# Loading each raw weight block one step ahead, in front of the W12 loads, in the seven-product stretches

## The chip, the cores and the metric

One core of one Trainium2 chip runs the kernel. The metric is the device time of one execution in microseconds, as a median of several runs. A profiled execution gives the trace that the rows below come from. TensorE is called PE here, VectorE DVE, ScalarE ACT, GpSimd POOL and SyncE SP. SP computes nothing: it issues nearly all loads, in the order in which they are written for it, and an instruction that has to wait holds up those behind it.

## The reference, cut to what matters

Two layers over 512 tokens of width 2048: a latent-attention layer and an mLSTM layer. The change touches the input projection of the second alone:

```python
proj = x @ w_in                      # x (512, 2048), w_in (2048, 8208), float32
qk, v, o, gates, z = jnp.split(proj, [o1, o2, o3, o4], axis=-1)
...
return (hcell * jax.nn.silu(z)) @ w_out
```

`v` (values), `o` and `z` (two gates) are 2048 columns wide each. Two of the four 512-column blocks of `v`, and all of `o` and `z`, come out of the function that the diff changes.

## The kernel before, in words

**Arithmetic.** A float32 product is made from three products of a shorter format. `split` (L166) cuts a tile into a high part, copied by ACT (L168), and a low part, which DVE gets by subtraction (L169). `mm3` (L206) then issues high x high, high x low and low x high, each a 128x128 by 128x512 matmul at L203.

**Seven products for eight.** `quad` (L298) computes 512 tokens by two 512-column blocks, c0 and c1, in the manner of Strassen and Winograd. The 2048 rows of the weights are taken in pairs of 128-row blocks, an even and an odd one. W11 is the even block at c0, W12 the even one at c1, W21 and W22 the odd ones at c0 and c1. Seven products (q1 to q7) of these, or of sums of these, with sums of the tokens' blocks replace eight. It is called five times in a row: once for `v`, then for each of four pairs of `o` and `z` blocks. In the time of the trace the five calls run from 819.6 to 1225.7 us.

**Stretches and steps.** A call has three stretches, each a loop over `i` = 0, 2, 4, 6, so of four steps. A step loads one raw block (`raw`, L315 to L320: 128 x 1024 floats, 512 KB, issued at L319) and works on it:

- first stretch (L355 to L363): W11 is the raw block. DVE adds W12 to it into a tile `t` (L360, two halves). q1 takes the split of W11, q5 that of `t`. `right` (L322 to L328) loads W12 as two tiles `e` of 256 KB (L327).
- second stretch (L371 to L379): W22 is the raw block, and W12 is loaded again. DVE adds W22 to W12 in place (L374, two halves) and to `t` (L376, two halves). q7 takes the split of the first sum, q6 that of `t`, q3 that of W22.
- third stretch (L398 to L404): W21 is the raw block. DVE adds it to `t` (L401, two halves). q2 takes the split of W21, q4 that of `t`. No W12 here.

A product of one step is 12 matmuls, so a step is 24, 36 or 24 matmuls, and a call 336.

**Buffers.** There are three raw buffers (`N_RAW`, L43), three of high and of low parts (`N_HI`), four `e` tiles (`N_E`, L42), hence room for the W12 of two steps, and 16 `t` tiles. A raw buffer comes free when its split at L169 and the additions that read it are done; an `e` tile after L360 in the first stretch and after its split in the second; a split's buffers after the product that reads them.

**Order.** The program text is not the order on the chip. The compiler's scheduler writes a fixed order for each engine and for SP, by the order of the program, by when it reckons that inputs are there, and by which buffer comes free. Each engine then takes its own list strictly in that order. `behind` (L160) adds an edge by which one instruction must be put later than another on the same engine, without a wait. Results that leave a call (`self.pending`, `some`) are put out during later steps: L382 to L407, with L999 to L1004 in the calls for the gates.

Of the kernel before, what the change touches and what calls it, by code (L numbers as in the profile page):

```python
# [17 lines left out]
P = 128  # L18
# [63 lines left out]
class Kern:  # L82
# [215 lines left out]
    def quad(self, w, c0, c1, x, S, done):  # L298

        nc = self.nc
        V = nc.vector
        n = KT // 2
        a, b = self.banks  # L310
        self.banks = b, a
        two = lambda f: [f(), f()]
        half = lambda v, j: v[:, 512 * j : 512 * j + 512]

        def raw(par, i, c):  # L315

            t = self.rt()
            src = w[2 * i * P : (2 * i + 4) * P, c : c + 512].rearrange("(k q p) c -> p q k c", p=P, q=2)
            nc.sync.dma_start(t.rearrange("p (k c) -> p k c", k=2), src[:, par])  # L319
            return t  # L320

        def right(i):  # L322

            t = two(self.e)
            for j in range(2):
                kt = 2 * (i + j)
                nc.sync.dma_start(t[j], w[kt * P : (kt + 1) * P, c1 : c1 + 512])  # L327
            return t  # L328

        def taken(t):  # L330
            hi, lo = self.wh(), self.wl()
            self.split(t, hi, lo)
            return hi, lo

        def taken2(t):
            hi, lo = self.wh(), self.wl()
            for j in range(2):
                self.split(t[j], half(hi, j), half(lo, j))
            return hi, lo

        def mul(ps, op, j, i, hl):

            for d in range(2):
                o = op(i + d)
                for m in range(2):
                    s = slice(j * 256 + m * P, j * 256 + (m + 1) * P)
                    self.mm3(ps[m], (o[0][:, s], o[1][:, s]), (half(hl[0], d), half(hl[1], d)),
                             i + d == 0, i + d == n - 1)
                self.tick()

        xe, xo = (lambda i: x[2 * i]), (lambda i: x[2 * i + 1])
        se, so = (lambda i: S[i][0]), (lambda i: S[i][1])
        q1, q5 = two(a), two(a)
        t = []
        for i in range(0, n, 2):  # L355
            w11 = raw(0, i, c0)
            t.append([self.t(), self.t()])
            w12 = right(i)
            for j in range(2):
                V.tensor_tensor(t[-1][j], half(w11, j), w12[j], op=ALU.add)  # L360
            mul(q1, xe, 0, i, taken(w11))
            mul(q5, so, 1, i, taken2(t[-1]))
            self.some(2)  # L363
        e1, e5 = two(self.t), two(self.t)
        for m in range(2):
            nc.scalar.copy(e1[m], q1[m])
        for m in range(2):
            nc.scalar.copy(e5[m], q5[m])

        q7, q6, q3 = two(b), two(a), two(b)  # L370
        for i in range(0, n, 2):  # L371
            w22, w12 = raw(1, i, c1), right(i)
            for j in range(2):
                V.tensor_tensor(w12[j], w12[j], half(w22, j), op=ALU.add)  # L374
            for j in range(2):
                V.tensor_tensor(t[i // 2][j], t[i // 2][j], half(w22, j), op=ALU.add)  # L376
            mul(q7, se, 1, i, taken2(w12))
            mul(q6, se, 0, i, taken2(t[i // 2]))
            mul(q3, so, 0, i, taken(w22))  # L379
        u, c12 = two(self.t), two(self.t)  # L380
        for m in range(2):
            V.tensor_tensor(u[m], q6[m], e1[m], op=ALU.add)  # L382

        def sums(m):
            V.tensor_tensor(e5[m], e5[m], u[m], op=ALU.subtract)
            V.tensor_tensor(u[m], u[m], q7[m], op=ALU.add)

        def upper(m):
            V.tensor_tensor(c12[m], e5[m], q3[m], op=ALU.add)
            done(m, 1, c12[m])  # L390

        def lower(m):
            V.tensor_tensor(e5[m], e5[m], q7[m], op=ALU.subtract)
            done(2 + m, 1, e5[m])

        self.pending += [partial(f, m) for f in (sums, upper, lower) for m in range(2)]
        q2, q4 = two(a), two(a)
        for i in range(0, n, 2):  # L398
            w21 = raw(1, i, c0)
            for j in range(2):  # L400
                V.tensor_tensor(t[i // 2][j], t[i // 2][j], half(w21, j), op=ALU.add)  # L401
            mul(q2, xo, 0, i, taken(w21))
            mul(q4, xo, 1, i, taken2(t[i // 2]))
            self.some(2)  # L404

        def left(tb, v, q):
            V.tensor_tensor(v, v, q, op=ALU.add)  # L407
            done(tb, 0, v)

        self.pending += [partial(left, c + m, v[m], q[m]) for c, v, q in ((0, e1, q2), (2, u, q4)) for m in range(2)]  # L410
# [764 lines left out]
```

## Time and profile before

| what | value |
|---|---|
| median of 3 runs | 1675.4 us (1674.34 to 1676.42) |
| the profiled execution, its own time | 1674.64 us |
| its span, first to last instruction | 1672.9 us |
| PE busy | 1619.4 us, 97% of the span |
| DVE busy | 1096.3 us, 66% |
| ACT busy | 742.3 us, 44% |
| DMA in the five calls, mean busy share | 0.57, 137 GB/s |

The time of an execution is a little longer than its span. A busy share is an average over stages; PE's is high everywhere, so what can be won or lost in a stage is PE's idle time there and the time that it runs at a lower clock. In a row of a timeline the start, the length, the engine, the line and the operation with what it writes and reads are followed by a count and, in brackets, by how long the engine was idle before and what ended this. `wlo` and `whi` are low and high parts of weights, `raw` the raw block, `e` W12, `t` the sums. "SPq" is SP's queue of loads.

### The profile page before, as it was taken

The numbers are of one execution on the slowest core, as the hardware profiler recorded it, in microseconds if no ns is written. First come the engines' busy times: TensorE is split into PE (matmuls) and PEld (weight loads), VectorE is DVE, ScalarE is ACT, GpSimd is POOL, SyncE is SP. The second block draws the span as 40 slices with busy tenths as digits, with TensorE's granted clock in tenths as the row PEclk, the third lists the DMA queues.
The fourth block names the chain that finished last, engine by engine and source line by source line (L and its number), as shares of the span: only waits on it lengthen the run. The fifth ranks groups of instructions, "written<-read, shape, count | busy, mean of one in ns | idle before, by whom it ended". The sixth has DMA issues, their size and how long they took to land.

```text
span 1672.9 us, 20587 instructions
## 1 busy us (share of the span) xinstructions
PE 1619.4 (97%) x7465; PEld 1339.6 (80%) x7465; DVE 1096.3 (66%) x1944; ACT 742.3 (44%) x1208; POOL 108.9 (7%) x236
## 2 busy tenths in 40 slices
PE   8999999999999999999999999999999999889996
PEld 6888888888888888778887877887788888778775
DVE  3375222577778535889577786977777756565777
ACT  3343222454556323345343444644445666654332
POOL 1000000000001000110001000000011111121000
PEclk9999999999999999999999999999999999989999
DMA  7333333322224236768646485548455745553565
GB/s 204 112 97 95 95 101 91 97 61 68 64 67 133 82 122 203 250 194 183 188 111 191 120 159 111 178 114 163 78 132 153 121 124 157 174 154 123 176 228 174
DMA packets 172263, 227.94 MB, mean 136 GB/s; under 512 B 23753, under 2 KB 97545, under 8 KB 172161
## 3 DMA queue, kind: packets, MB, share of 16 engines
q1 hardware_dynamic: 163696, 202.02, 45.2%
q0 software_dynamic: 8464, 24.62, 4.7%
q8 instruction: 58, 0.95, 0.2%
q14 instruction: 45, 0.36, 0.1%
HBM read 205.44 MB, written 18.92 MB: 134 GB/s over the span
## 4 chain that ended last, share of the span: by engine, by line
PE 77%; DVE 11%; DMA 8%; issue 2%; ACT 1%; POOL 1%; SPq 0%; DVEq 0%; POOLq 0%; ACTq 0%
PE acc L203 61%; PE ps L203 14%; DMA raw<-in_ml_w_in_dram 5%; DVE wlo L169 5%; PE ps L200 2%; DMA raw<-in_ml_w_out_dram 1%; DMA e<-in_ml_w_in_dram 1%; DVE t L401 1%; ACT whi L168 1%; DVE t L407 1%; DVE t L360 1%; DVE t L1074 1%; POOL s L263 0%; DVE t L1073 0%; DVE t L1003 0%
## 5 line engine op out<-in xcount | busy, mean ns | idle before, releaser
L203 PE MATMUL acc<-whi,h 128*128 128x512 f32 x1656 | 533.3, 395 | 5.1 <-ACT whi L168 4.0
L169 DVE TENSOR_TENSOR wlo<-raw,whi 128x1024 fp32r<-128x1024 f32 (+1 forms) x291 | 349.3, 1202 | 266.4 <-ACT whi L168 260.4
L168 ACT CAST whi<-raw 128x1024 fp32r<-128x1024 f32 (+2 forms) x295 | 303.6, 1029 | 454.9 <-PE acc L203 344.2
L203 PE MATMUL acc<-h,whi 128*128 128x512 f32 x1536 | 472.2, 392 | 0.0
L203 PEld LDWEIGHTS acc<-whi,h 128*128 128x128 f32 x1656 | 313.7, 190 | 70.7 <-ACT whi L168 4.8
L203 PE MATMUL acc<-wlo,h 128*128 128x512 f32 x828 | 326.8, 395 | 9.6 <-DVE wlo L169 9.5
L203 PEld LDWEIGHTS acc<-h,whi 128*128 128x128 f32 x1536 | 286.1, 188 | 58.0 <-issue 1.0
L203 PE MATMUL acc<-h,wlo 128*128 128x512 f32 x736 | 287.4, 390 | 0.0
L203 PEld LDWEIGHTS acc<-wlo,h 128*128 128x128 f32 x828 | 157.2, 190 | 44.6 <-DVE wlo L169 13.6
L203 PEld LDWEIGHTS acc<-h,wlo 128*128 128x128 f32 x736 | 138.5, 188 | 29.8
L203 PE MATMUL ps<-whi,h 128*128 128x512 f32 x488 | 158.1, 396 | 0.0
L203 PEld LDWEIGHTS ps<-whi,h 128*128 128x128 f32 x488 | 93.8, 192 | 19.8
L203 PE MATMUL ps<-wlo,h 128*128 128x512 f32 x244 | 98.0, 401 | 9.5 <-DVE wlo L169 9.5
L168 ACT CAST whi<-t 128x512 fp32r<-128x512 f32 x120 | 68.6, 619 | 84.9 <-PE ps L203 44.8
L169 DVE TENSOR_TENSOR wlo<-t,whi 128x512 fp32r<-128x512 f32 x120 | 77.4, 685 | 16.4 <-ACT whi L168 16.4
L203 PE MATMUL acc<-whi,v 128*128 128x512 f32 x248 | 84.4, 399 | 0.0
L200 PE MATMUL ps<-ident,t 128*128 128x128 f32 x352 | 56.9, 284 | 13.4 <-DMA t<-in_x_dram 6.5
L200 PEld LDWEIGHTS ps<-ident,t 128*128 128x128 f32 x352 | 44.4, 145 | 26.6 <-ACT t L929 7.7
L203 PEld LDWEIGHTS ps<-wlo,h 128*128 128x128 f32 x244 | 46.7, 192 | 23.2 <-DVE wlo L169 13.3
L703 ACT ACTIVATE t<-ps,s 128x128 f32<-128x128 f32 (+3 forms) x64 | 33.8, 528 | 67.9 <-DVE s L702 67.8
L203 PE MATMUL ps<-h,h 128*128 128x128 f32 (+3 forms) x288 | 61.9, 327 | 0.0
L203 PEld LDWEIGHTS acc<-whi,v 128*128 128x128 f32 x248 | 46.6, 188 | 10.3
(213 smaller groups left out, 1751.5 us busy)
## 6 DMA issues: line engine op xcount, KB each, us to landing
raw<-in_ml_w_in_dram SPq DMA_DIRECT2D x116, 512.0 KB, 5.1
raw<-in_mla_w_in_dram SPq DMA_DIRECT2D x48, 512.0 KB, 3.8
raw<-in_mla_w_out_dram SPq DMA_DIRECT2D x48, 512.0 KB, 4.1
raw<-in_ml_w_out_dram SPq DMA_DIRECT2D x48, 512.0 KB, 4.5
e<-in_ml_w_in_dram SPq DMA_DIRECT2D x80, 256.0 KB, 4.3
t<-in_x_dram SPq DMA_DIRECT2D x32, 256.0 KB, 5.3
raw<-in_mla_w_kvb_dram SPq DMA_DIRECT2D x16, 256.0 KB, 3.2
raw<-in_mla_w_kvb_dram SPq DMA_DIRECT2D x32, 128.0 KB, 2.4
```

The lines of the kernel that those rows point to most:

```text
L168: a = self.nc.scalar.copy(hi, src)
L169: b = self.nc.vector.tensor_tensor(lo, src, hi.bitcast(F32), op=ALU.subtract)
L200: self.nc.tensor.transpose(out, in_, ident)
L203: self.nc.tensor.matmul(out, lhsT, rhs, start=start, stop=stop)
L360: V.tensor_tensor(t[-1][j], half(w11, j), w12[j], op=ALU.add)
L401: V.tensor_tensor(t[i // 2][j], t[i // 2][j], half(w21, j), op=ALU.add)
L407: V.tensor_tensor(v, v, q, op=ALU.add)
L703: nc.scalar.activation(pt[bi], s[:, :n], AF.Exp, bias=b, scale=scale, accum_out=tot)
L1074: nc.vector.scalar_tensor_tensor(t, t, moments[tb][1], b, op0=ALU.mult, op1=ALU.add)
```

## The change

`raw` now notes each load that it begins. A list of the call's twelve raw blocks, in the order of use, is worked off by `next_raw`, which begins blocks until two are under way and hands out the first: at each step the block of the next step is begun, across the borders of the stretches, but not across calls. In `right`, each load of W12 gets an edge that puts it behind the raw load begun last, that is behind the next step's raw block, in SP's order. Buffers, sizes and arithmetic stay as they are.

```diff
-            nc.sync.dma_start(t.rearrange("p (k c) -> p k c", k=2), src[:, par])
+            begun.append(nc.sync.dma_start(t.rearrange("p (k c) -> p k c", k=2), src[:, par]))
             return t
+
+        ahead, begun = [], []
+        order = [(0, c0), (1, c1), (1, c0)]
+        order = [(par, i, c) for par, c in order for i in range(0, n, 2)]
+
+        def next_raw():
+
+            while order and len(ahead) < 2:
+                ahead.append(raw(*order.pop(0)))
+            return ahead.pop(0)
 
         def right(i):
 
             t = two(self.e)
             for j in range(2):
                 kt = 2 * (i + j)
-                nc.sync.dma_start(t[j], w[kt * P : (kt + 1) * P, c1 : c1 + 512])
+                self.behind([nc.sync.dma_start(t[j], w[kt * P : (kt + 1) * P, c1 : c1 + 512])], begun[-1:])
             return t
...
-            w11 = raw(0, i, c0)
+            w11 = next_raw()
...
-            w22, w12 = raw(1, i, c1), right(i)
+            w22, w12 = next_raw(), right(i)
...
-            w21 = raw(1, i, c0)
+            w21 = next_raw()
```

## Rows read from the trace of the kernel before

**Rows 1.** The page, part 4: the chain that ended last, by engine.

```profile
PE 77%; DVE 11%; DMA 8%; issue 2%; ACT 1%; POOL 1%; SPq 0%; DVEq 0%; POOLq 0%; ACTq 0%
```

**Rows 2.** Stretches, one per call: length, busy PE, PEld, DVE, ACT, POOL; clock; DMA.

```profile
819.60:896.90 77.30, 77.00 (x338) 63.00 (x336) 60.33 (x89) 34.59 (x51) 2.98 (x6) 1.00 0.56 155
896.90:978.30 81.40, 78.48 (x337) 64.11 (x336) 61.81 (x91) 37.73 (x54) 2.16 (x4) 0.98 0.54 140
978.30:1063.60 85.30, 79.75 (x337) 63.81 (x337) 64.61 (x96) 40.09 (x59) 2.16 (x4) 0.98 0.63 140
1063.60:1141.00 77.40, 77.17 (x337) 62.95 (x337) 63.86 (x95) 39.90 (x59) 2.16 (x4) 1.00 0.57 146
1141.00:1225.70 84.70, 80.67 (x338) 64.79 (x337) 61.60 (x92) 39.58 (x59) 5.25 (x18) 0.96 0.55 109
```

**Rows 3.** Timeline of PE, third call: the matmul behind the longest gap.

```profile
999.07 0.50 PE L203 MATMUL ps<-wlo,h 128*128 128x512 f32 x1 [3.16 <-DVE wlo L169]
```

**Rows 4.** The stretch behind that gap, columns as in rows 2.

```profile
999.10:1003.40 4.30, 4.30 (x12) 3.39 (x13) 4.13 (x7) 0.59 (x1) 0.00 (x0) 0.60 0.66 120
```

**Rows 5.** Timeline of DVE around the start of the third call.

```profile
968.85 1.22 DVE L169 TENSOR_TENSOR wlo<-raw,whi 128x1024 fp32r<-128x1024 f32 x1
...
976.27 0.69 DVE L360 TENSOR_TENSOR t<-raw,e 128x512 f32<-128x512 f32 x1 [3.20 <-DMA raw<-in_ml_w_in_dram]
976.88 1.22 DVE L169 TENSOR_TENSOR wlo<-raw,whi 128x1024 fp32r<-128x1024 f32 x1
...
980.42 0.69 DVE L360 TENSOR_TENSOR t<-raw,e 128x512 f32<-128x512 f32 x1
...
997.19 0.69 DVE L374 TENSOR_TENSOR e<-e,raw 128x512 f32<-128x512 f32 x1 [2.98 <-DMA raw<-in_ml_w_in_dram]
997.80 1.22 DVE L169 TENSOR_TENSOR wlo<-raw,whi 128x1024 fp32r<-128x1024 f32 x1
998.93 0.69 DVE L374 TENSOR_TENSOR e<-e,raw 128x512 f32<-128x512 f32 x1
```

**Rows 6.** Timeline of ACT, the high part of the split of rows 3.

```profile
990.28 1.06 ACT L168 CAST whi<-raw 128x1024 fp32r<-128x1024 f32 x1 [1.61 <-PE ps L203]
```

**Rows 7.** Waits in the five calls: who waited for what: us, times, longest.

```profile
DVE e L374 <- DMA raw<-in_ml_w_in_dram: 15.4, 7, 4.2
...
DVE t L360 <- DMA raw<-in_ml_w_in_dram: 10.8, 4, 3.2
```

**Rows 8.** Waits of SP's queue before the raw loads, columns as in rows 7.

```profile
SPq L319 <- DVE wlo L169: 250.4, 58, 9.4
```

**Rows 9.** Timeline of SP's loads: end of the second call, start of the third.

```profile
937.30 0.93 SPq L327 DMA_DIRECT2D e<-in_ml_w_in_dram  x2
...
965.35 0.37 SPq L319 DMA_DIRECT2D raw<-in_ml_w_in_dram  x1
...
970.09 0.37 SPq L319 DMA_DIRECT2D raw<-in_ml_w_in_dram  x1
970.69 6.63 SPq L327 DMA_DIRECT2D e<-in_ml_w_in_dram  x4
...
987.68 0.33 SPq L327 DMA_DIRECT2D e<-in_ml_w_in_dram  x1
988.82 0.38 SPq L319 DMA_DIRECT2D raw<-in_ml_w_in_dram  x1
```

**Rows 10.** The chain that ended last, in order of time: start, us, what.

```profile
937.63 5.52 PE ps L203 x24
...
988.82 8.25 DMA raw<-in_ml_w_in_dram
```

**Rows 11.** W12 pairs issued from 970.7 (third call) and 1056.6 us (fourth), to landing.

```profile
DMA to landing us min/median/max: 6.6/7.3/7.9
...
DMA to landing us min/median/max: 5.0/5.1/5.1
```

**Rows 12.** Two raw loads of the first call, issued at 800.4 and 805.9 us, to landing.

```profile
DMA to landing us min/median/max: 4.7/4.9/5.1
```

## The prediction

> **What bounds the kernel now.** I read the page first: PE holds 77% of the chain that ended last, DVE 11% and loads 8% [rows 1]. So a change to the loading order can only be worth what the matrix engine loses while it waits. The second view is the table of stretches, one line for each of the five calls of `quad` [rows 2]. The reader is to see that all five issue the same 336 or 337 matmuls, yet take 77.30, 81.40, 85.30, 77.40 and 84.70 us. The calls with almost no idle PE, the first and the fourth, give the floor, 77.3 us. Above it the second, third and fifth lose 4.1 + 8.0 + 7.4 = 19.5 us, 1.2% of the kernel. This is the most that the change can give. PE's idle time (length less busy) is 0.30, 2.92, 5.55, 0.23 and 4.03 us, 13.0 in all; the rest is mostly the clock.
>
> Where does it sit? In the third call PE stops 3.16 us before 999.07, released by the subtraction that makes `wlo` (L169) [rows 3], and right behind it the granted clock is 0.60 on average over 4.30 us [rows 4], so mostly at the lower of its two levels (1.2 and 2.4 GHz): some 4.3 x 0.4 = 1.7 us more. The three calls that lose time are also the three whose clock is below 1.00 [rows 2]. The timeline of DVE tells why [rows 5]: the raw split that PE wants ran at 997.80, behind an L374 that stood idle 2.98 us for a raw block. ACT had its half of that split at 990.28 + 1.06 = 991.34 [rows 6]. DVE takes its instructions in the order written for it, and that order holds additions for a later step ahead of a split that is due now. This is the pattern: **a load that comes late stops not its own product but the split behind it.** In the five calls L374 waited 15.4 us for raw blocks, 7 times [rows 7].
>
> **What the change does.** No instruction is added or removed: 12 raw loads and 16 loads of W12 a call, the same sizes, on the same queue (SP's); POOL's and ACT's queues are not touched. What moves is the order of SP.
>
> *The raw loads.* They are asked for a step earlier in the program. But SP waited before L319 for the raw split 58 times, 250.4 us [rows 8]: with three raw buffers, block k+3 is issued when the split of block k ends, in the rows shown within 0.05 us (split 968.85 + 1.22 = 970.07, load 970.09) [rows 5, 9]. A place further forward in the queue can't free a buffer. I cost this edit at nothing, between a gain of about 2 us (the few blocks that now stand behind a W12 load) and no loss.
>
> *The W12 loads.* These do move. W12 of step k now stands behind raw k+1, which needs a free raw buffer. Before, they had four buffers of their own and ran up to two steps ahead; in the third stretch SP fetched those of the next call at 937.30, while the second raw block of that call left only at 965.35 [rows 9]. Now the first W12 of a call leaves behind that block, some 28 us later, and every other pair of the first stretch directly behind the raw block that the last split freed. So W12 goes from early to just in time. Behind the new wait on SP stand the next raw load and its W12; the first to feel it is DVE's addition L360 (L374 in the second stretch), then the raw split behind that on DVE, then PE.
>
> **The price of one step.** In the first stretch PE uses two products a step: 24 matmuls, 5.52 us [rows 10]. What DVE and SP need for one step, if L360 stands ahead of the next raw split (it does at 976.27, before the split at 976.88 [rows 5]): from the end of a raw split to the issue of W12 0.60 us (970.09 to 970.69 [rows 9]); to its landing 5.0 us at the least (fourth call) and 6.6 for the first of the pair in the third [rows 11]; one L360, 0.69, and the split, 1.22 [rows 5]. That makes 7.5 to 9.1 us against 5.52. I count one addition, since the second half of that pair stands behind the split (980.42 [rows 5]).
>
> A reserve softens it: a raw split can begin when the product three back ends. ACT starts with its gap closed by PE and takes 1.06, DVE 1.22 [rows 5, 6], about 2.4 with the hand-over, of two products' 5.52: 3.1 us are left. **Check on before:** in the third call the four steps from the split ending at 970.07 to that ending at 999.02 took 28.95 us; 4 x 5.52 + 3.1 = 25.2, so 3.8 us of idling should come out, and 3.16 stand in one gap [rows 3].
>
> **The sum.** Four such steps in each of the calls two to five (the first starts with its W12 long there): 4 x 7.5 - 25.2 = 4.8 us idle a call at the low price, 4 x 9.1 - 25.2 = 11.2 at the high. I take the middle, 8.0, as one call shows the low price and one the high: 32 us. From it goes what these four calls idle now, 12.7 us, of which I leave 2 that lie in other stretches: 32 - 10.7 = 21.3 more. Not each step will have its addition ahead of the split: about a tenth off, 19. In the second stretch three products stand over a step (8.3 us), so most hides; its cover is the three products, and without it the pair would cost as above. I put 1 us for each of four calls, 4, between 0 and 8. The clock: a gap of 3 us brought 1.7; where 13 us of idling lowered it in three calls, I expect two more such places, 3.4, between 0 and 7. Raw blocks of the third stretch lose the W12 of the next call that ran beside them: -0.5. In all 19 + 4 + 3.4 - 0.5 = **26 us**. The profiled execution took 1674.64 us (span 1672.9 and 1.7 around it), 0.76 under the median of 1675.4; 1674.64 + 26 is 1700.6, against the median **1701**. The low price everywhere gives (4 x 4.8 - 10.7) + 0 + 0 - 2 = +6.5, 1682; the high (44.8 - 10.7) + 8 + 7 = +49, 1724.
>
> **Rivals.** *Faster (0.27).* The additions that wait for W12 are the very ones that block DVE now. If W12 comes later in the compiler's reckoning too, L374 of a later step may be placed behind the raw split instead of ahead, and the gaps of calls two, three and five go. It decides at one point: which of the two, the addition or the split, stands first on DVE in the first stretch. For it speaks that after each gap the second L374 already stands behind the split (997.80, 998.93 [rows 5]); against it that L376 needs the raw block alone and can take L374's place, and that L360 and L374 stood ahead of the split at 976.27 and 997.19 in one call. If all goes, 19.5 us; more likely four fifths, -16, hence 1659.
>
> It has a second leg, the landing of the raw block itself: 8.25 us at 988.82 with a W12 load issued 1.1 us before it [rows 9, 10], against 4.7 to 5.1 for two blocks with none close [rows 12]. A W12 pair still follows each block, and the pair of the last step still precedes it by a step, so I see little of this gap given back. The Trainium skill, "DMA: Bandwidth & Descriptors", section "Queues, rings and completion order", says that each DMA engine consumes descriptors in ring order, while a later one may finish before an earlier one; by that a raw block in front of its W12 would be fetched first. By that rule the result is this rival's 1659. The trace bears it out in half: the block issued at 970.09 was there by 976.27 and its W12 only 6.6 us after 970.69, in the order of issue [rows 5, 9, 11]; but it had DVE wait 3.20 us all the same.
>
> *No change (0.11).* The reserve of 3.1 us and the idle buffers swallow the later W12: each addition stands behind the split, but L376, in L374's place, still waits for raw. The change then has done only half of what it says, since no raw block began sooner. Time 1675, 3 either way.
>
> **Chances.** My forecast, slower, has 0.62, as the raw loads' release is plain in the rows and the W12 can only come later; what I can't see is the new order on DVE. A measurement of this kernel can tell about 0.2%, 3.4 us, from no change. Faster by more: 0.27; within: 0.11; slower: 0.62. The range reaches from the faster rival's middle, 1661, to just under the high price, 1722; the forecast's own is 1682 to 1722.
>
> **What would show it.** Right: SP still issues each raw load at the end of a raw split; W12 of a call's first step leaves behind the second raw block; DVE waits at L360 for W12 with a raw split behind it (now its waits there, 10.8 us, end with raw blocks [rows 7]); PE's idle time in calls two to five grows from 12.7 to about 32 us, with more places at the lower clock. Wrong: raw loads issued before the split three back ends; the `quad` lines of the table all near 77.3 us; or additions behind the splits and DVE idle where PE is not.

## The result, and the profile after

The changed kernel took **1687.13 us** (median of 4 runs, 1685.68 to 1687.41), the kernel before beside it 1674.87 (4 runs, 1673.30 to 1676.42): ratio 1.0074, 95% interval 1.0063 to 1.0086, 12.3 us slower. The prediction had the sign, and the time lies in its range, but its price, 26 us, is twice the true one.

The table of stretches after, one line a call, columns as in [rows 2]:

```profile
819.00:896.10 77.10, 77.02 (x338) 63.07 (x336) 58.33 (x85) 34.58 (x51) 2.97 (x6) 1.00 0.54 144
896.10:978.60 82.50, 79.15 (x337) 64.06 (x336) 61.15 (x90) 37.77 (x54) 2.16 (x4) 0.98 0.55 138
978.60:1069.60 91.00, 79.82 (x338) 62.38 (x337) 67.67 (x100) 40.33 (x59) 2.16 (x4) 1.00 0.63 131
1069.60:1146.20 76.60, 76.60 (x337) 63.11 (x336) 60.63 (x90) 39.89 (x58) 2.16 (x4) 1.00 0.56 149
1146.20:1236.60 90.40, 80.84 (x337) 63.60 (x337) 64.94 (x96) 39.78 (x60) 5.26 (x18) 0.98 0.59 113
```

Against [rows 2] the five calls are 417.6 us long instead of 406.1, so 11.5 of the 12.3 us are in them. PE's busy time in them is 393.4 against 393.1 us: no work was added and none slowed down on balance; the new time is idle PE, 24.2 us instead of 13.0. And it is not spread: the second call gained 1.1 us, the fourth lost 0.8, the third is 5.7 longer and the fifth 5.7.

The waits of SP's queue before the raw loads, for [rows 8], are as many as they were, but longer, 339.9 us instead of 250.4:

```profile
SPq L319 <- DVE wlo L169: 339.9, 58, 11.6
```

The chain that ended last, for [rows 1], adds up to half the span only, so it was not followed further back, and its shares can't be set against the 77% of PE there; in what it covers, loads have a third of PE's share, where they had a tenth:

```profile
PE 27%; DMA 9%; DVE 8%; issue 3%; ACT 2%; POOL 1%; SPq 0%; POOLq 0%; DVEq 0%; ACTq 0%
```

Now the third and fifth call alone, cut at the places where PE goes from the first stretch (two products a step) to the second (three) and on to the third. First the changed kernel, first and second stretch of the third call, then of the fifth:

```profile
978.60:1007.90 29.30, 23.55 (x98) 17.66 (x97) 22.65 (x34) 12.66 (x20) 2.16 (x4) 1.00 0.88 178
1007.90:1047.80 39.90, 34.48 (x145) 26.67 (x144) 25.38 (x38) 13.96 (x21) 0.00 (x0) 1.00 0.46 81
...
1146.20:1174.70 28.50, 23.29 (x98) 17.66 (x97) 22.67 (x34) 12.65 (x21) 2.16 (x4) 1.00 0.86 173
1174.70:1214.90 40.20, 35.85 (x146) 27.94 (x145) 25.41 (x38) 13.92 (x21) 1.19 (x12) 0.96 0.46 83
```

The same four stretches of the kernel before:

```profile
978.30:1006.10 27.80, 24.18 (x98) 19.06 (x98) 23.01 (x36) 12.64 (x20) 2.16 (x4) 0.94 0.83 173
1006.10:1041.90 35.80, 33.87 (x145) 26.76 (x144) 21.93 (x32) 13.79 (x21) 0.00 (x0) 1.00 0.49 101
...
1141.00:1169.50 28.50, 25.14 (x98) 19.80 (x97) 23.40 (x36) 12.56 (x20) 2.16 (x4) 0.88 0.83 171
1169.50:1203.80 34.30, 33.64 (x146) 26.82 (x145) 21.14 (x31) 13.80 (x21) 1.19 (x12) 1.00 0.39 71
```

The first stretches grew by 1.5 and 0.0 us, the second ones by 4.1 and 5.9. The prediction had put 19 us into the first stretches and 4 into the second. PE's idle time (length less busy) did grow in the first stretches, from 3.62 to 5.75 us and from 3.36 to 5.21; but the clock there was 1.00 instead of 0.94 and 0.88, so that PE's busy time fell by 2.5 us and hid most of it.

**What waits in the second stretch.** The timeline of DVE after, second stretch of the third call, DVE's first additions for it and its last steps (L411, the addition of the third stretch, was L401; L384 was L374, L386 was L376):

```profile
1002.95 0.69 DVE L384 TENSOR_TENSOR e<-e,raw 128x512 f32<-128x512 f32 x1 [0.85 <-DMA e<-in_ml_w_in_dram]
...
1009.36 1.33 DVE L384 TENSOR_TENSOR e<-e,raw 128x512 f32<-128x512 f32 x2 [1.16 <-DMA e<-in_ml_w_in_dram]
...
1023.86 1.22 DVE L169 TENSOR_TENSOR wlo<-raw,whi 128x1024 fp32r<-128x1024 f32 x1
...
1031.22 0.69 DVE L411 TENSOR_TENSOR t<-t,raw 128x512 f32<-128x512 f32 x1 [4.94 <-DMA raw<-in_ml_w_in_dram]
...
1033.04 1.34 DVE L384 TENSOR_TENSOR e<-e,raw 128x512 f32<-128x512 f32 x2
1034.29 0.68 DVE L411 TENSOR_TENSOR t<-t,raw 128x512 f32<-128x512 f32 x1
1034.89 1.22 DVE L169 TENSOR_TENSOR wlo<-raw,whi 128x1024 fp32r<-128x1024 f32 x1
```

The timeline of SP's loads beside it:

```profile
1025.11 0.38 SPq L319 DMA_DIRECT2D raw<-in_ml_w_in_dram  x1
1025.53 0.94 SPq L337 DMA_DIRECT2D e<-in_ml_w_in_dram  x2
```

Read the last steps first, together with SP. The raw split ends at 1023.86 + 1.22 = 1025.08, SP sends the next raw load at 1025.11, and DVE, after the low parts of an `e` pair, comes to the addition that reads this very block: it can start only at 1031.22, 6.1 us later. Behind it stand the low parts of a `t` pair, the two additions L384, its own second half, and only then the next raw split, which ends at 1036.11 and lets the next load go (1036.14). So although there are three raw buffers, one load at a time is under way, because **DVE's order has the addition of a block ahead of the split of the block two before it**, and that split is what frees the buffer for the block that comes after. One turn of this ring is a landing plus DVE's work: 1025.08 to 1036.11, 11.0 us, against the 8.3 that PE needs for a step. The kernel before had the same ring, but shorter; the same view of it:

```profile
1026.11 0.69 DVE L401 TENSOR_TENSOR t<-t,raw 128x512 f32<-128x512 f32 x1 [4.25 <-DMA raw<-in_ml_w_in_dram]
...
1028.53 1.22 DVE L169 TENSOR_TENSOR wlo<-raw,whi 128x1024 fp32r<-128x1024 f32 x1
...
1035.17 0.69 DVE L401 TENSOR_TENSOR t<-t,raw 128x512 f32<-128x512 f32 x1 [4.21 <-DMA raw<-in_ml_w_in_dram]
```

From addition to addition 9.06 us. The difference is the pair L384 (1.34 us) which now stands inside the ring, as its W12 comes with the late raw block, and a longer landing. Only one of the turns that grew is of this kind. From raw split to raw split the four turns of this stretch take 12.1, 10.8, 11.0 and 8.6 us, before 10.3, 11.3, 9.1 and 9.1. In the first, DVE waits for W12 of the step itself (L384 at 1002.95 and 1009.36, 2.3 us with a short wait between them), where in the kernel before it waited 1.0 us for loads. In the fifth call the same two turns grew, by 2.0 and 1.8 us. That the ring exists already before the change is something the prediction had not seen: it had the wait of L374 in [rows 7], but read it as single gaps.

The waits of DVE in the five calls of the changed kernel answer [rows 7] (who waited for what: us, times, longest):

```profile
DVE t L411 <- DMA raw<-in_ml_w_in_dram: 35.1, 10, 4.9
DVE t L370 <- DMA e<-in_ml_w_in_dram: 29.8, 14, 4.7
...
DVE e L384 <- DMA e<-in_ml_w_in_dram: 16.6, 14, 3.8
```

L370 (L360 before) now waits for W12 and no more for raw blocks, as foretold.

### The profile page after: what moved, and what is told of

Same layout as the page of the kernel before. It is cut to its first block, busy times and chain, and to the rows that moved or that the text cites. A ratio compares the mean times of both kernels' runs of the same rounds, so it can differ in the third digit from the quotient of the medians.

```text
span 1685.2 us, 20508 instructions
## 1 busy us (share of the span) xinstructions
PE 1619.7 (96%) x7465; PEld 1338.3 (79%) x7465; DVE 1096.6 (65%) x1944; ACT 742.9 (44%) x1208; POOL 109.9 (7%) x236
## 4 chain that ended last, share of the span: by engine, by line
PE 27%; DMA 9%; DVE 8%; issue 3%; ACT 2%; POOL 1%; SPq 0%; POOLq 0%; DVEq 0%; ACTq 0%
PE acc L203 19%; PE ps L203 7%; DMA e<-in_ml_w_in_dram 4%; DVE wlo L169 4%; DMA raw<-in_ml_w_in_dram 2%; DMA raw<-in_ml_w_out_dram 1%; DMA e<-vscr 1%; ACT whi L168 1%; POOL s L263 1%; DVE t L386 1%; DVE t L411 1%; DVE e L384 0%; PE ps L200 0%; DMA gscr<-h 0%; DVE t L417 0%
## 5 line engine op out<-in xcount | busy, mean ns | idle before, releaser
L203 PE MATMUL ps<-wlo,h 128*128 128x512 f32 x244 | 97.0, 397 | 14.6 <-DVE wlo L169 14.2
L169 DVE TENSOR_TENSOR wlo<-t,whi 128x512 fp32r<-128x512 f32 x120 | 77.3, 685 | 15.6 <-ACT whi L168 15.6
L200 PE MATMUL ps<-ident,t 128*128 128x128 f32 x352 | 57.0, 285 | 14.2 <-DMA t<-in_x_dram 6.5
```

Source lines behind the costliest of these rows:

```text
L169: b = self.nc.vector.tensor_tensor(lo, src, hi.bitcast(F32), op=ALU.subtract)
L200: self.nc.tensor.transpose(out, in_, ident)
L203: self.nc.tensor.matmul(out, lhsT, rhs, start=start, stop=stop)
```

## The experiments

Each was timed in five rounds beside the kernel before, whose medians there lie between 1673.57 and 1674.60 us. The theory at the start was only "the loss sits in the second stretch".

**1. Raw blocks asked for early, no rule on W12.** Against the changed kernel:

```diff
-  self.behind([nc.sync.dma_start(t[j], ...)], begun[-1:])
+  nc.sync.dma_start(t[j], ...)
```

> The changed kernel without the rule that W12 leaves behind the raw block begun last: the raw blocks are still asked for a step ahead in the program. Theory (a raw load leaves when a raw split frees its buffer, wherever it stands in the queue): the time before, 1675 us within 2, with the five calls' PE idle time near 13 us. Rival A (asking a step earlier does bring the blocks sooner): 1660 to 1670. Rival B (asking ahead is itself what costs, since it moves loads out of their place): 1684 to 1688.

Measured: 1674.60 us, ratio 1.0001 (0.9992 to 1.0010). Half of the change does nothing; the rule that W12 leaves behind the newest raw block does all of it. The reason is not the one of the theory, though, and the run is no test of it. Compared by what each instruction writes and reads, the two traces have the same order on PE, DVE, ACT and POOL, and on SP two neighbouring loads at 813 us, ahead of the five calls, trade places: the compiled program is nearly that of the kernel before. That an earlier place in the queue does not bring a block sooner has to be read from the changed kernel, whose loads do stand in a new order.

**2 and 3. The rule in one stretch only.** `right(i)` gets a second argument; in 2 it is true in the first stretch, in 3 in the second:

```diff
-  self.behind([nc.sync.dma_start(t[j], ...)], begun[-1:])
+  self.behind([nc.sync.dma_start(t[j], ...)], begun[-1:] if edge else [])
```

> The rule on W12 in the first stretch of each call only (W12 of the first stretch behind the raw block begun last; W12 of the second stretch free). Theory (the loss sits in the second stretch, whose PE idle time grew by 10 of the 11.7 us in the profile after): 1675 to 1678 us. Rival (my prediction's sum: the first stretch has just-in-time W12 and carries most of it, 19 of 26): 1684 to 1690.

Measured: 1684.47 us, 1.0061 (1.0049 to 1.0074).

> The rule on W12 in the second stretch of each call only. Theory (the loss sits there): 1683 to 1688 us, with the second stretches of calls three and five at 39 to 41 us and those of the other calls at 33. Rival (the first stretch carries it): 1675 to 1679. Second rival (neither part alone loses much, the order of DVE's instructions that the two make together does): both this and the kernel with the first stretch alone under 1680.

Measured: 1680.23 us, 1.0041 (1.0027 to 1.0055).

Both cost, and together (10.2 + 5.9 = 16.1 us against the medians beside them) more than the whole change, so "the loss sits in the second stretch" fell. Run 2 lies in the range of its rival, the prediction's own sum, but the time does not go only where the rule stands: with the rule in the first stretch only, the second stretch of the third call is longer too, 37.4 us instead of 35.8; with it in the second only, the first stretch of that call is 2.5 us *shorter*. First the kernel with the rule in the first stretch, both stretches of the third call:

```profile
977.50:1008.10 30.60, 24.42 (x98) 19.01 (x97) 23.66 (x36) 12.96 (x20) 2.16 (x4) 0.94 0.87 177
1008.10:1045.50 37.40, 34.77 (x145) 28.09 (x144) 24.38 (x36) 13.80 (x21) 0.00 (x0) 0.95 0.45 79
```

then that with the rule in the second:

```profile
976.70:1002.00 25.30, 22.74 (x97) 17.80 (x97) 18.91 (x29) 12.59 (x20) 2.16 (x4) 1.00 0.77 165
1002.00:1043.10 41.10, 34.77 (x146) 26.60 (x145) 26.45 (x39) 13.93 (x21) 0.00 (x0) 1.00 0.53 106
```

What differs between all these kernels, beside SP's order, is where the compiler put the additions on DVE. That became the new theory, with "W12 that comes late costs by itself" as its rival.

**4. W12 behind the raw block of its own step**, one block earlier than in the change:

```diff
-  self.behind([nc.sync.dma_start(t[j], ...)], begun[-1:])
+  self.behind([nc.sync.dma_start(t[j], ...)], begun[-2:-1])
```

> The rule on W12 one block weaker: W12 leaves behind the raw block of its own step instead of the next one's. SP's order of loads comes out almost as in the changed kernel (four of 489 places differ), DVE's order differs from it in some 40 places. If the later W12 on SP's queue is what costs, whatever DVE's order: 1684 to 1688 us, as the changed kernel. If the order of DVE's instructions is what costs (an addition that waits for a load ahead of a raw split): it goes with DVE's order and lies elsewhere, 1672 to 1680.

Measured: 1676.12 us, 1.0013 (1.0004 to 1.0021). This run tells less than was hoped. The four places understate what moved on SP: the pattern repeats, and by them W12 leaves one raw block earlier all through a call. Both orders differ, so the run can't choose between the theories. It does show that leaving one block earlier is worth some 10 us to the compiled kernel as a whole (1.8 us over the kernel before beside it, where the change has 12.3).

**5. The additions put late, on the kernel before.** Every addition that reads raw block k (L360, L374, L376, L401) is put behind the low half of the raw split of block k-2 on DVE. The rule orders instructions on one engine; nothing else is changed in the program:

```diff
+  splits = []
   def taken(t):
-      self.split(t, hi, lo)
+      splits.append(self.split(t, hi, lo)[1])
+  def after_split(*args, **kw):
+      a = V.tensor_tensor(*args, **kw)
+      self.behind([a], splits[-2:-1] if len(splits) >= 2 else [])
...
-  V.tensor_tensor(t[-1][j], half(w11, j), w12[j], op=ALU.add)
+  after_split(t[-1][j], half(w11, j), w12[j], op=ALU.add)
```

and so at the three other places.

> The kernel before with one rule on DVE's order: the additions of block k (all that read a raw block) stand behind the raw split of block k-2. Theory (a raw load leaves only when a raw split ends; where DVE does the addition of block k ahead of the split of block k-2, it waits for a load that was issued only when the split before it ended, so that one load at a time is under way and a step costs landing plus DVE's work, 9 to 11 us): 1655 to 1665 us, second stretches all near 33 us. Rival A (the loads themselves are slow in calls three and five and no order helps): 1670 to 1676. Rival B (additions that wait for splits come too late for their own products): over 1676.

Measured: **1656.78 us, 0.9899** (0.9885 to 0.9912), as the theory had it; the second stretches are at 33.0 us in all five calls. In what was compiled, SP's order differs in 22 of 567 places too and ACT's in 13 of 1208, so this run alone does not show that DVE's order does it.

**6. The same on the changed kernel.**

> The changed kernel with the same rule on DVE's order. Theory (what the change cost it cost through DVE's order): the loss goes and the time comes near that of the kernel before with the rule, 1655 to 1670. Rival (W12 that leaves later costs by itself): 1680 to 1687.

Measured: 1676.74 us, 1.0016 (1.0007 to 1.0025). Some 9 of the 12.3 us of the change's loss are gone (3.2 are left against the kernel before beside it), but the run ends between the two accounts: with additions two blocks behind, DVE still waits 57 us for the late W12 in the five calls. This is the cleanest pair of all: by the two traces SP, ACT, POOL and PE have exactly the changed kernel's order, so the 9 us are DVE's order alone.

**7. One block stricter, on the kernel before**: additions of block k behind the split of block k-1 (`splits[-1:]`).

> The kernel before with the additions of block k behind the raw split of block k-1, one block stricter. If the theory holds and the products have the reserve: 1655 to 1665, as with the weaker rule. If an addition that is that late holds up its own product (Rival B of the weaker rule): 1665 to 1690.

Measured: **1652.36 us, 0.9872** (0.9857 to 0.9886), the fastest of all and under the range of 1655 to 1665, 21 us under the kernel before and some 34 under the changed one. Its first, third and fifth call, columns as in [rows 2] (the second and fourth are 76.70 us too):

```profile
817.60:894.30 76.70, 76.70 (x338) 63.08 (x337) 61.88 (x90) 34.59 (x51) 4.07 (x8) 1.00 0.57 154
...
971.00:1047.60 76.60, 76.60 (x337) 63.03 (x336) 64.20 (x95) 39.78 (x58) 2.16 (x4) 1.00 0.72 156
...
1124.30:1201.00 76.70, 76.70 (x338) 63.10 (x337) 61.21 (x91) 39.35 (x59) 5.26 (x18) 1.00 0.66 125
```

PE is busy from end to end at a granted clock of 1.00 (2.4 GHz). Its DVE timeline in the second stretch of the third call (L338 is the new helper) shows the ring broken:

```profile
1002.53 1.23 DVE L169 TENSOR_TENSOR wlo<-raw,whi 128x1024 fp32r<-128x1024 f32 x1 [1.88 <-ACT whi L168]
1003.67 1.29 DVE L338 TENSOR_TENSOR e<-e,raw 128x512 f32<-128x512 f32 x2
1004.87 1.29 DVE L338 TENSOR_TENSOR t<-t,raw 128x512 f32<-128x512 f32 x2
...
1010.88 1.23 DVE L169 TENSOR_TENSOR wlo<-raw,whi 128x1024 fp32r<-128x1024 f32 x1 [1.94 <-ACT whi L168]
```

Split to split takes 8.35 us, PE's own 8.3; the additions behind a split find their block there and wait for nothing, and DVE waits for ACT's half of the split instead, which waits for PE. SP's order of loads came out different here as well; run 9 leaves it as it was.

**8. The stricter rule on the changed kernel.** SP's loads stand in exactly the changed kernel's order.

> The changed kernel with the stricter rule on DVE's order (additions of block k behind the raw split of block k-1). SP's queue holds its loads in exactly the changed kernel's order, W12 late included; only DVE's order differs. If the change cost what it cost through additions that stand on DVE ahead of a raw split: 1650 to 1660 us, as the kernel before with that rule (1652.4). If W12 that leaves late costs by itself even then: 1665 to 1680.

Measured: **1660.04 us, 0.9917** (0.9902 to 0.9932), at the upper end of the first account. With the change's own loading order 27 us are won back by DVE's order (ACT's differs in some places too, the other engines' not at all). The rest, 1660.0 against the 1652.4 of run 7, is what W12 costs by itself when it leaves late, under this order of DVE: the first stretches of the third and fifth call are 26.6 and 25.6 us where run 7 has 21.9 in both, all others at the floor. DVE's waits name it:

```profile
DVE t L348 <- DMA e<-in_ml_w_in_dram: 17.6, 10, 3.4
DVE e L348 <- DMA e<-in_ml_w_in_dram: 6.2, 5, 2.7
```

**9 and 10. Which additions.** The stricter rule on the kernel before, for the two additions of the second stretch only (9; SP's order is that of the kernel before, ACT's differs in places as DVE's does), and for the first and third stretch only (10).

> The kernel before with the stricter rule for the additions of the second stretch only (the two that read a block of W22). SP's order is exactly that of the kernel before. The longest gaps of before stood behind an addition of the second stretch, done ahead of a raw split at the end of the first. Theory: most of the gain of the full rule (-21 us), 1653 to 1662. Rival (the additions of the first and third stretch hold as much): 1664 to 1672.

Measured: 1654.46 us, 0.9876 (0.9858 to 0.9894).

> The kernel before with the stricter rule for the additions of the first and third stretch only; those of the second stay as they were placed. Theory: little of the gain, 1668 to 1676 us. Rival: half or more of it, 1652 to 1664.

Measured: 1665.57 us, 0.9945 (0.9929 to 0.9961). The first came out as the theory had it; the second won more than its 1668 to 1676, and the two gains (20.1 and 9.0 us) sum to more than that of the full rule. The stretches of the third call say why. In run 9 both are near the floor; in run 10 the first is at the floor and the second is slower than in the kernel before (35.8):

```profile
973.10:994.90 21.80, 21.80 (x97) 17.98 (x96) 18.78 (x29) 12.41 (x20) 2.16 (x4) 1.00 1.02 208
994.90:1033.60 38.70, 35.18 (x146) 28.01 (x145) 25.31 (x38) 13.86 (x21) 0.00 (x0) 0.96 0.58 118
```

So the additions of the second stretch, done too early, cost time in both stretches; mending the first stretch alone hands part of the wait on to the second.

**11. Pairs of columns swapped.** In the kernel before, `for pair in (1, 0, 3, 2)`. Why do the third and fifth call lose most?

> The kernel before with the four pairs of column blocks taken in the order 1, 0, 3, 2 (the calls two to five of the seven-product routine). If the columns that a block lies in decide how long its loads take: the second and fourth calls now have the raw loads of 5 to 8 us and lose 7 to 8 us each, the third and fifth those near 4.2 us; the total stays within 3 us of 1675. If the place in the program decides (other transfers beside them): the third and fifth stay the slow ones.

Measured: 1677.45 us, 1.0022 (1.0010 to 1.0033). The loads issued in the second to fifth call of the kernel before (KB each, median us to landing):

```profile
raw<-in_ml_w_in_dram SPq DMA_DIRECT2D x13, 512.0 KB, 4.3
```

```profile
raw<-in_ml_w_in_dram SPq DMA_DIRECT2D x13, 512.0 KB, 5.4
```

are the second and third call; the fourth has 4.4 and the fifth 5.5. In the swapped kernel the same four calls have 5.4, 4.5, 5.5 and 4.4. The second, third and fifth of them (the fourth takes 85.40 us), columns as in [rows 2]:

```profile
896.60:986.80 90.20, 81.91 (x338) 65.34 (x337) 61.75 (x92) 37.91 (x54) 2.16 (x4) 0.94 0.60 132
986.80:1064.30 77.50, 76.92 (x337) 62.94 (x336) 63.79 (x95) 39.93 (x58) 2.16 (x4) 1.00 0.56 146
...
1149.70:1226.40 76.70, 76.70 (x338) 63.06 (x337) 61.06 (x91) 39.31 (x59) 5.26 (x18) 1.00 0.41 115
```

The slow loads go with the columns, not with the place in the program, and the loss goes with the slow loads, although PE, DVE, ACT and POOL have the same order in the two kernels (SP differs in three places). That fits the ring, whose turn hangs on the landing, and is the likely reason why the change costs 5.7 us in one call and nothing in the next. In the fourth call after, two turns took 8.8 and 8.9 us (split ends at 1094.90, 1103.69 and 1112.60), little over the 8.3 of a step, and PE had no wait; the same two in the third took 10.8 and 11.0. What it is about those columns stays open.

Not tried: a fourth raw buffer, the direct way to let a load go before a split ends. Nor was the changed order of SP run with the DVE order of the kernel before, so how much of the 12.3 us is the late W12 and how much the compiler's new order of DVE stays open.

## Why the prediction was right and wrong

**Raw loads no sooner: right.** All 56 raw loads issued in the five calls after stand at most 0.08 us behind the end of a raw split (1025.08 and 1025.11 above), though SP's order is a new one. Run 1 (1.0001) does not show it, since its loads kept the order of before.

**W12 becomes just in time: right.** W12 of the third call's first step left behind the second raw block, as the timeline of SP after shows, some 28 us later than in [rows 9]:

```profile
959.67 5.91 SPq L319 DMA_DIRECT2D raw<-in_ml_w_in_dram  x2
965.64 0.93 SPq L337 DMA_DIRECT2D e<-in_ml_w_in_dram  x2
```

**The first stretch, +19: this step failed.** Measured, the first stretches of the third and fifth call grew by 1.5 us in all, that of the second by 0.7, and that of the fourth got 0.7 shorter. Without the clock it is more, but still far from 19: PE's idle time in these four stretches went from 10.1 to 14.2 us, where the sum had some 30. The fault is "four such steps in each of the calls", with "about a tenth off" for additions that stand behind the split. The count was wrong more than the price: in the third call the four steps, from raw split to raw split, took 11.7, 5.9, 5.3 and 9.2 us, in the fifth 10.3, 5.9, 5.4 and 9.6, so that two of four ran near PE's pace and two were above the high price of 9.1; in the fourth call none was near it. The timeline of DVE after, first stretch of the fourth call:

```profile
1065.99 0.69 DVE L370 TENSOR_TENSOR t<-raw,e 128x512 f32<-128x512 f32 x1 [1.41 <-DMA e<-in_ml_w_in_dram]
1066.60 1.22 DVE L169 TENSOR_TENSOR wlo<-raw,whi 128x1024 fp32r<-128x1024 f32 x1
...
1070.14 0.68 DVE L370 TENSOR_TENSOR t<-raw,e 128x512 f32<-128x512 f32 x1
...
1076.08 1.28 DVE L370 TENSOR_TENSOR t<-raw,e 128x512 f32<-128x512 f32 x2
...
1077.89 1.22 DVE L169 TENSOR_TENSOR wlo<-raw,whi 128x1024 fp32r<-128x1024 f32 x1
```

Of the four steps this one waits 1.41 us and the first 0.75; the pair at 1076.08 and the next find their W12 there. That at 1076.08 left with the split that ended at 1067.82, and another raw split has run since: the addition is not due at the next split after its W12 left, as I had it, but at the one behind that. From the split ending at 1067.82 to that ending at 1079.11 two steps take 11.3 us, 5.6 each, near PE's own 5.52, where I had 7.5 at the least. And where a W12 addition did stop DVE (4.40 us at 997.27, third call), it stood in the place of a gap that the kernel before had already (3.16 us, [rows 3]). Run 8, where the late W12 is all that is left, puts its price at 4.7 + 3.7 us, in two calls.

**The second stretch, +4 (0 to 8): this step failed too.** 4.1 + 5.9 = 10.0 us, in two calls rather than four. The failing part is the cover of three products (8.3 us a step), which was to hide most of it: in the third call the ring of split, raw load, addition, split took 9.1 us already in the kernel before, so there was no cover left. What grew is in part W12 of the step itself, at the beginning of the stretch, and in part the ring, which the late pair L384 made longer. Looking at [rows 7] I had priced the wait of single additions; I had not asked what the load that they waited for had itself been waiting for.

**The clock, +3.4: the wrong way.** Length times the missing share of the clock, summed over the five lines, is some 3.5 us after, where [rows 2] gives some 6.7 (an estimate, as the column is rounded): more idle time in PE came with less time at the lower level. PE's busy time rose by 0.4 us in all even so.

**The third stretch, -0.5:** at most a few tenths either way (+0.4 in the second call); the third and fifth calls' third stretches have the same length to 0.1 us.

**The sign and the range.** W12 that came late did cost time, as forecast. That the time lies inside the range is in part luck: most of the 19 us was not there, the second stretches took 6 us more than the 4 put on them, and the clock went the other way.

**The rivals.** The faster one asked the right question, which of addition and split stands first on DVE: run 8 against the changed kernel shows it to be worth 27 us. But the change did not move the additions behind the splits; it took the wait for raw to the wait for W12 in one place and put the early L386, which reads raw alone, in L374's place in another, as the text had feared: at 909.14 an L386 waits 3.73 us for a raw block with a raw split right behind it. In the fourth call the rival did come true (77.4 to 76.6 us).

**The ceiling, 19.5 us, was a little low:** run 7 brings all five calls to 76.7 us instead of 77.3, 22.7 us under [rows 2].

The rule of the Trainium skill on ring order ("DMA: Bandwidth & Descriptors", "Queues, rings and completion order"), by which the faster rival's raw block in front would be fetched first, did not bring that rival's time. The order on SP was as the change wanted it, the blocks still left no sooner, and no run here shows that a raw block in front of its W12 lands faster (median 5.5 us in the third call after, as 5.4 before). The trace agrees on the other side only: W12 behind a raw block took longer to land, a median of 6.8 us in that call where it had been 5.4. No run here separates this from other causes. (The prediction puts this rival at 1659 us where it prices it and at 1661 where it gives the range; nothing hangs on it.)

## What to carry over

Where a load is released by a use of its buffer, follow the ring: what frees the buffer, what that instruction stands behind on its own engine, and what the instruction in front waits for. If that is the load just released, the extra buffers are idle, and an earlier place in the queue does not help; putting the consumers behind the instruction that frees the buffer does (here -1.3%). And when a change moves loads, the compiler's new order on the consuming engine can be worth more than the loads: read it before pricing each step alike.

## What was not expected of the hardware

The landing of a raw block (512 KB) goes with the columns that it is read from: 4.3 to 4.5 us for two pairs and 5.4 to 5.5 for the other two, whatever their place in the program (run 11).

The clock did not follow the length of a gap in PE's work. In the changed kernel PE stopped 2.86 us before 1165.60 and 2.51 us before 1180.40, both in the fifth call. Two stretches behind these gaps, the first from the end of its gap, the second from 1.3 us after the end of its own, columns as in [rows 2]:

```profile
1165.60:1169.00 3.40, 3.01 (x12) 2.18 (x12) 3.40 (x5) 0.70 (x2) 0.00 (x0) 1.00 0.92 181
1181.70:1185.10 3.40, 3.40 (x10) 2.64 (x9) 1.63 (x4) 0.69 (x2) 0.35 (x4) 0.50 0.57 90
```

The granted clock was 1.00 behind the longer one and 0.50, the lower level, behind the shorter. In the third call 11.2 us of idle PE in many gaps left it at 1.00, where [rows 4] had 0.60 behind one gap of 3.16 us. So the clock can't be counted per gap, as the prediction did.
